# Natural-layout input-projection groups taken two at a time: 512 columns to a PSUM bank, nine buffers of split weights

## The chip, the cores and the metric

The program runs on one core of a Trainium2 chip. The metric is the device time of one execution in microseconds (us), the median of several runs. The profile page and the trace come from one further, profiled execution of the same program.

## The reference

One block of a streaming encoder is computed for 1024 tokens of width 1024, in float32. One input projection feeds three mixers (stick-breaking attention, retention, a Conformer convolution), one output projection and an MLP follow.

```python
h = rms_norm(x, mix_norm_g[l])
u = jnp.einsum('btd,dc->btc', h, w_in[l])            # 1024 -> 3328 columns
sb_q, sb_k, sb_v, r_q, r_k, r_v, r_g, c_a, c_gate = jnp.split(u, split_at, axis=-1)
q = to_heads(rms_norm(sb_q per head of 64), 4); k likewise; v = to_heads(sb_v, 4)
y_sb = from_heads(stick_breaking_attention(q, k, v))
rq = retention_rotary(to_heads(r_q, 8), pos)
rk = retention_rotary(to_heads(r_k, 8), pos) * (HEAD_DIM ** -0.5)
ret = rms_norm(from_heads(multiscale_retention(rq, rk, rv)) per head)
y_ret = jax.nn.silu(r_g) * ret
y_conv = conformer_conv(c_a, c_gate, ...)            # GLU, 31 taps, LayerNorm, silu
x = x + jnp.einsum('btc,cd->btd', concat([y_sb, y_ret, y_conv]), w_out[l])
h = rms_norm(x, mlp_norm_g[l])
x = x + relu(h @ w_ff1[l]) ** 2 @ w_ff2[l]
```

## The kernel before

Every large product is made of three matmuls of a faster float32 form (f32r): each operand is split into a rounded part `hi` and the rest `lo`, and `mm3` adds hi times hi, hi times lo and lo times hi into one PSUM bank. So each weight that comes from memory (`wraw`, 128x512) is first cast on ACT (`whi`, L160) and then subtracted on POOL or DVE (`wlo`, L161). There are `WB` = 6 buffers of each.

The input projection has 13 groups of 256 columns. The first (`qk0`, queries and keys of attention heads 0 and 1) is computed while x arrives and fills all eight banks. Two (`cv0`, `cv1`) are computed in transposed layout, 512 tokens to a bank. The other ten are in natural layout: 128 tokens by 256 columns, eight token tiles `tt` a group, 8 k-steps of 3 matmuls each, in the order v, qk1, then (after the convolution groups) k0, v0, g0, q0, k1, v1, g1, q1. `gemm_group` makes one such group. A token tile fills half a bank of tag "g"; there are two banks of this tag. When the tile is done a function `evac` reads the bank, and only then can the tile after next begin in it: `v_evac` (L307, L308) for v, `sb_norm` and then `sb_turn` for qk1, `rotary` for k and q (two DVE operations L501 and L503, two POOL operations L505 and L506), a copy on ACT for v0 and v1, a sigmoid on ACT and L668 on DVE for g, `ret_chunk` for q.

`ret_chunk` (L586 on) makes one 128-token chunk of retention of four heads: `rotary`, then, a tick later, transposes of k and q on PE (L598, L600) and three copies of them on ACT (L601, L604); scores on PE (L609), masked on DVE (L610); the output on PE (L620, L621) and the state (L627 on PE, L633 or L637 on DVE); a norm; two transposes back (L653).

Small work is laid beside the projection by a count of ticks: `at_tick(t, order, fn)` puts a step at a tick, `tick(gemm)` runs the steps of that tick and then one piece of projection. In before a tick is one token tile of 24 matmuls (of a convolution group one half of a bank, 12 matmuls of 512 columns). A group has 8 ticks: v 0 to 7, qk1 8 to 15, the convolution groups 16 to 31, k0 32 to 39 and so on, to q1 88 to 95. Attention heads begin at tick 1. The 124 convolution taps (`conv_tap`, L533, DVE, 128x512 each) are laid over ticks from 41 on by the list `per`: one a tick for 12 ticks, three for 11, two for 8, then three. A scheduler orders each engine's instructions at build time, starting from this order.

The normalisation factor `rstd` is known only after `qk0` is complete: 8 small matmuls (L224), `mse` on DVE (L225), `rstd` on POOL (L175). Then `sb_norm` of pair 0 runs once for each of the 8 token tiles, each with a POOL operation `rs` (L175) and a DVE multiply into `cv` (L277). `sb_turn` (L284 to L300) transposes four tiles at a time for the attention heads, which begin with z matmuls (L327 to L330), sigmoids on ACT and a scan on DVE (L340).

The weights of the MLP (`wr`, 128x1024, loaded at L828) have four buffers of tag "wr"; one of them serves as `state` of retention until it is over. Three loads of them are issued by SP at the start of the program.

## Time and profile before

| | |
|---|---|
| median of 3 runs | 1163.6 us (1163.55 to 1165.37) |
| profiled execution | 1164.28 us |
| its span in the trace | 1162.5 us |
| PE busy | 1132.3 us (97% of the span) |
| DVE busy | 871.3 us (75%) |
| ACT, POOL busy | 487.5 us, 530.5 us |

The span is the time from the first to the last instruction of the trace; 1.78 us of the profiled execution lie around it, and the median of the runs is 0.68 us below the profiled execution. PE is the engine of the matmuls (TensorE), DVE is VectorE, ACT ScalarE, POOL GpSimd, SP the engine that issues most transfers. Busy time of PE includes the modelled tail of each matmul, so the start-to-start distance of matmuls says more than their own duration.

### The profile page before, as it was taken

Reading aid. Unit: us, or ns where it says so; the run is one execution under the profiler, and the core shown is the slowest. Engines: PE = TensorE matmul, PEld = TensorE weight load, DVE = VectorE, ACT = ScalarE, POOL = GpSimd, SP = SyncE. Lnnn points to the kernel's source line nnn. Section 1 sums busy time; section 2 is a strip of 40 time slices with the busy share of each in tenths; the row PEclk is TensorE's granted clock in tenths of the full one; section 3 lists DMA queues with packets and bytes.
Section 4 is the critical chain, followed back from the end, with each engine's and each line's share of the span. In section 5 each row is a group of like instructions: output and inputs, shape, how many; then the busy total and the mean of one; then the engine's idle time right before and its main releaser. Section 6 shows DMA issues by size and latency. Waiting matters only on the chain.

```text
span 1162.5 us, 17630 instructions
## 1 busy us (share of the span) xinstructions
PE 1132.3 (97%) x6376; PEld 986.6 (85%) x6376; DVE 871.3 (75%) x1355; ACT 487.5 (42%) x921; POOL 530.5 (46%) x432
## 2 busy tenths in 40 slices
PE   7999999999999999999999999999879999999998
PEld 7998889999999998787888888888658888888887
DVE  6786766769987987788966756575588897896964
ACT  7575644442322252555433333343334344344442
POOL 3565535436761562342565655556462442521300
PEclk9999999999999999999999999999989999999999
DMA  8111111112121142212444444453586564553332
GB/s 286 38 37 37 55 29 42 41 55 65 56 65 37 55 182 55 71 66 91 152 146 146 164 141 163 144 163 127 213 311 220 164 212 136 158 183 85 109 129 89
DMA packets 63735, 137.11 MB, mean 118 GB/s; under 512 B 7201, under 2 KB 11937, under 8 KB 63649
## 3 DMA queue, kind: packets, MB, share of 16 engines
q1 hardware_dynamic: 63072, 135.56, 35.5%
q8 instruction: 50, 0.82, 0.3%
q10 hardware_dynamic: 576, 0.44, 0.1%
q14 instruction: 37, 0.29, 0.1%
HBM read 98.22 MB, written 37.75 MB: 117 GB/s over the span
## 4 chain that ended last, share of the span: by engine, by line
PE 84%; DVE 9%; DMA 3%; issue 2%; ACT 1%; SPq 0%; POOL 0%; DVEq 0%; ACTq 0%; POOLq 0%
PE g L116 12%; PE g L118 12%; PE g L117 12%; PE t L117 5%; PE t L118 5%; PE t L116 5%; PE o L117 5%; PE o L116 5%; PE o L118 4%; PE z L117 4%; PE z L118 4%; PE z L116 4%; DVE DM__508_2651 L533 3%; PE o L374 2%; PE t L355 1%
## 5 line engine op out<-in xcount | busy, mean ns | idle before, releaser
L161 DVE TENSOR_TENSOR wlo<-sum,whi 128x512 fp32r<-128x512 f32 x78 | 75.5, 971 | 84.5 <-ACT whi L160 84.5
L161 POOL TENSOR_TENSOR wlo<-wraw,whi 128x512 fp32r<-128x512 f32 x57 | 87.1, 1544 | 77.3 <-ACT whi L160 77.2
L160 ACT CAST whi<-sum 128x512 fp32r<-128x512 f32 x78 | 48.1, 618 | 112.9 <-POOL sum L831 48.1
L161 DVE TENSOR_TENSOR wlo<-wr,whi 128x512 fp32r<-128x512 f32 x80 | 76.6, 963 | 10.0 <-ACT whi L160 9.0
L344 POOL TENSOR_TENSOR be<-be,kp 128x512 f32<-128x512 f32 (+3 forms) x48 | 46.0, 960 | 78.3 <-DVE kp L340 49.9
L160 ACT CAST whi<-wr 128x512 fp32r<-128x512 f32 x80 | 48.5, 620 | 65.5 <-PE t L117 20.8
L836 POOL TENSOR_TENSOR sum<-wr 128x512 f32<-128x512 f32 x16 | 23.2, 1452 | 114.1 <-DMA wr<-in_w_ff_dram 84.1
L160 ACT CAST whi<-wraw 128x512 fp32r<-128x512 f32 x68 | 41.8, 620 | 58.1 <-DMA wraw<-in_w_in_dram 23.5
L340 DVE TENSOR_TENSOR_SCAN kp<-kp 128x512 f32<-128x512 f32 (+3 forms) x48 | 51.1, 1067 | 10.5 <-ACT kp L333 10.0
L533 DVE SCALAR_TENSOR_TENSOR DM__508_2651<-glu,vec,DM__508_2651 128x512 f32<-128x512 f32 x60 | 54.3, 943 | 0.1
L175 POOL TENSOR_TENSOR rs<-ss,nhalf 128x4 f32<-128x4 f32 (+1 forms) x36 | 37.4, 1040 | 30.1 <-DVE ss L641 15.4
L533 DVE SCALAR_TENSOR_TENSOR glu<-glu,vec 128x512 f32<-128x512 f32 x60 | 47.5, 853 | 0.0
L831 POOL TENSOR_TENSOR sum<-wr,sum 128x512 f32<-128x512 f32 x19 | 33.9, 1786 | 11.2 <-DVE wlo L161 11.2
L333 ACT ACTIVATE kp<-z 128x512 f32<-128x512 f32 (+3 forms) x48 | 23.6, 494 | 16.7 <-PE z L330 13.0
L831 POOL TENSOR_TENSOR sum<-sum,wr 128x512 f32<-128x512 f32 x18 | 24.9, 1384 | 11.3 <-DVE wlo L161 11.3
L116 PE MATMUL g<-whi,xh__12_100 128*128 128x256 f32 x82 | 25.3, 309 | 2.8 <-DVE P__107_556 L308 0.9
L334 ACT ACTIVATE be<-z 128x512 f32<-128x512 f32 (+3 forms) x48 | 23.5, 493 | 5.0 <-PE t L355 5.0
L118 PE MATMUL g<-whi,xl__53_362 128*128 128x256 f32 x82 | 23.3, 286 | 1.6 <-DVE xl__53_362 L195 1.6
L116 PE MATMUL g<-whi,xh__34_250 128*128 128x256 f32 x82 | 23.4, 286 | 0.9 <-ACT xh__34_250 L194 0.9
L355 PE MATMUL t<-ident,be 128*128 128x128 f32 x144 | 24.2, 274 | 0.1
L116 PE MATMUL g<-whi,xh__19_145 128*128 128x256 f32 x82 | 23.6, 288 | 0.0
L117 PE MATMUL g<-wlo,xh__19_145 128*128 128x256 f32 x82 | 23.6, 288 | 0.0
(2888 smaller groups left out, 4366.4 us busy)
## 6 DMA issues: line engine op xcount, KB each, us to landing
wr<-in_w_ff_dram SPq DMA_DIRECT2D x40, 512.0 KB, 3.9
wraw<-in_w_in_dram SPq DMA_DIRECT2D x52, 256.0 KB, 3.1
P__418_2109<-in_rot_dram SPq DMA_DIRECT2D x32, 128.0 KB, 2.0
wraw<-in_w_out_dram SPq DMA_DIRECT2D x16, 256.0 KB, 2.7
P__18_143<-in_xT_dram SPq DMA_DIRECT2D x1, 512.0 KB, 4.7
P__22_176<-in_xT_dram SPq DMA_DIRECT2D x1, 512.0 KB, 5.7
P__29_215<-in_xT_dram SPq DMA_DIRECT2D x1, 512.0 KB, 3.5
P__33_248<-in_xT_dram SPq DMA_DIRECT2D x1, 512.0 KB, 7.9
```

What stands on the lines that cost most here:

```text
L116: TE.matmul(out, lh, rh, start=start, stop=False, skip_group_check=on)
L117: TE.matmul(out, lh, rl, start=False, stop=False, skip_group_check=on)
L118: TE.matmul(out, ll, rh, start=False, stop=stop, skip_group_check=on)
L160: S.copy(hi, raw)
L161: (lo_engine or GP).tensor_tensor(out=lo, in0=raw, in1=hi.bitcast(F32), op=ALU.subtract)
L175: GP.tensor_tensor(out=out, in0=in_, in1=nhalf[:, 0:in_.shape[1]], op=ALU.pow)
L333: S.activation(kp[:, 0:n], pz[:, 0:n], AF.Sigmoid, scale=-0.125)
L340: V.tensor_tensor_scan(rev, rev, rev, kp[:, n:n + 1], op0=ALU.mult, op1=ALU.bypass)
L344: GP.tensor_tensor(out=be[:, 0:n], in0=be[:, 0:n], in1=kp[:, 1:n + 1], op=ALU.mult)
L355: TE.transpose(pt[:, j * P:j * P + P], be[:, j * P:j * P + P], ident)
L533: V.scalar_tensor_tensor(out=acc, in0=src, scalar=vec[:, o:o + 1], in1=acc, op0=ALU.mult, op1=ALU.add)
L831: (eng or GP).tensor_tensor(out=o, in0=x, in1=y, op=ALU.subtract)
```

## The change

Ten natural groups become five pairs: v with qk1, k0 with v0, g0 with q0, k1 with v1, g1 with q1. In a pair a weight chunk holds 256 columns of the one and 256 columns of the other group for one k-step, so `mm3` runs on 512 columns and fills a whole bank. A token tile takes two ticks (k-steps 0 to 3, then 4 to 7), so the pair has the same 16 ticks as the two groups had. When the tile is done, both groups' evacuations read their half of the bank.

- The eight chunks of a pair are made by `w_wide`. Nine buffers hold them: the six `whi`/`wlo`, and three 128x1024 tiles `ww` of tag "wr". The `lo` part alternates between DVE and POOL (in before it was on POOL). Raw chunks have five buffers instead of three.
- Before a pair ends, only its last token tile prepares the chunks of the next pair (one is prepared a tile earlier); the pair v with qk1 prepares none.
- Attention heads begin at tick 4 instead of 1, and the third head no longer waits for tick 18.
- `state` moves into a slot of the rotary tables (three slots instead of four for tables), and the buffers of the MLP weights become three of "wr" and one of "wq". The three early loads of MLP weights stand, in SP's order, behind the last rotary table and directly ahead of the eight loads of the residual x; in before they stood between the loads of x at the start.

```diff
-    sources = [d["w_in"][g, :, 512 * c:512 * c + 512] for g in range(len(GROUPS)) for c in range(4)]
+    sources = [d["w_in"][i] for i in range(4 * len(GROUPS))]
     sources += [d["w_out"][i] for i in range(2 * NK)]
     raws = {}
+    rawq = wp.tile([P, 2, 512], F32, tag="wq", name="rawq", bufs=1)
     wpos = [0, 0]
     def w_dma(upto):
         while wpos[0] < min(upto, len(sources)):
-            raw = wp.tile([P, 512], F32, tag="wraw", name=nm("wraw"), bufs=RAW)
+            n = wpos[0] % (RAW + 2)
+            raw = rawq[:, n - RAW, :] if n >= RAW else wp.tile([P, 512], F32, tag="wraw", name=nm("wraw"), bufs=RAW)
             nc.sync.dma_start(raw, sources[wpos[0]])
             raws[wpos[0]] = raw
             wpos[0] += 1
     halves = []
+    nwide = [0]
+
+    def w_wide():
+
+        c = wpos[1]
+        wpos[1] += 1
+        w_dma(c + RAW + (2 if c >= RAW else 0))
+        n = nwide[0] % 9
+        nwide[0] += 1
+        lo_engine = V if nwide[0] % 2 else GP
+        if n < WB:
+            return w_split(raws[c], lo_engine)
+        t = wp.tile([P, 1024], F32R, tag="wr", name=nm("ww"), bufs=3)
+        hi, lo = t[:, 0:512], t[:, 512:1024]
+        S.copy(hi, raws[c])
+        lo_engine.tensor_tensor(out=lo, in0=raws[c], in1=hi.bitcast(F32), op=ALU.subtract)
+        return hi, lo
     def w_part(lo_engine=None):
         if not halves:
             c = wpos[1]
             wpos[1] += 1
-            w_dma(c + RAW)
+            w_dma(c + RAW + (2 if c >= RAW else 0))
             hi, lo = w_split(raws[c], lo_engine)
             halves.extend((hi[:, 256 * h:256 * h + 256], lo[:, 256 * h:256 * h + 256]) for h in range(2))
         return halves.pop(0)
...
     pre = {"w": [], "due": None}
+    AHEAD = {(3, 0): 1}
+
     def gemm_group(evac, ahead=True):
+
         w = pre["w"]
         pre["w"] = []
         for tt in range(NT):
-            def run(tt=tt):
-                while len(w) < NK:
-                    w.append(w_part())
-                ps = bank("g")
-                ts = slice(tt * P, tt * P + P)
-                for k in range(NK):
-                    mm3(ps[:, 0:256], xh[k][:, ts], xl[k][:, ts], w[k][0], w[k][1], k == 0, k == NK - 1)
-                at_tick(now[0] + 1, 0, lambda: evac(tt, ps))
-                if ahead and 2 <= tt and len(pre["w"]) < 2 * WB - NK:
-                    pre["w"].append(w_part())
-            tick(run)
+            pb = {}
+            ts = slice(tt * P, tt * P + P)
+            for kh in range(2):
+                def run():
+                    if kh == 0:
+                        pb[0] = bank("g")
+                    for k in range(4 * kh, 4 * kh + 4):
+                        if len(w) <= k:
+                            w.append(w_wide())
+                        mm3(pb[0], xh[k][:, ts], xl[k][:, ts], w[k][0], w[k][1], k == 0, k == NK - 1)
+                    if ahead and len(pre["w"]) < AHEAD.get((tt, kh), 0):
+                        pre["w"].append(w_wide())
+                    while ahead and tt == NT - 1 and len(pre["w"]) < 4 + 4 * kh:
+                        pre["w"].append(w_wide())
+                tick(run)
+            at_tick(now[0], 0, lambda tt=tt, ps=pb[0]: evac(tt, ps))
     sb_prepare(0)
     mix_sb[0] = page(16)
-    pre["w"] = parts(2 * WB - NK)
     for tt in range(NT):
         sb_norm(0, tt, raw0[tt // 4][:, tt % 4, :])
         if tt % 4 == 3:
             sb_turn(0, tt // 4)
     for i in range(4):
         vst.append(page(12 + i, (P, 2, 4, P), F32R))
-    t1 = sb_head(0, 0, 1)
+    t1 = sb_head(0, 0, 4)
     t1 = sb_head(0, 1, t1)
-    t1 = sb_head(1, 0, max(t1, 18))
+    t1 = sb_head(1, 0, t1)
     sb_end = sb_head(1, 1, t1) + 4
-    gemm_group(v_evac)
     mix_sb[1] = page(17)
     sb_prepare(1)
-    def qk1_evac(tt, ps):
-        sb_norm(1, tt, ps[:, 0:256])
+    def vqk1_evac(tt, ps):
+        v_evac(tt, ps)
+        sb_norm(1, tt, ps[:, 256:512])
         if tt % 4 == 3:
             sb_turn(1, tt // 4)
-    gemm_group(qk1_evac)
+    gemm_group(vqk1_evac, ahead=False)
     rbc = slot("DM")
     at_tick(now[0], 6, lambda: row_bcast(rbc, rstd, "o"))
     glu = [None, None]
...
                         for k in range(4 * kh, 4 * kh + 4):
                             mm3(pb[j], w[k][0][:, cs], w[k][1][:, cs], xh[k][:, tsl], xl[k][:, tsl],
                                 k == 0, k == NK - 1)
-                        if hf == 1 and len(pre["w"]) < 2 * WB - NK:
-                            pre["w"].append(w_part())
+                        if hf == 1 and len(pre["w"]) < (2 * WB - NK if ct == 0 else 3) and (ct == 0 or (j, kh) != (1, 0)):
+                            pre["w"].append(w_part() if ct == 0 else w_wide())
                     tick(run)
             at_tick(now[0], 0, lambda a=(ct, hf, pb[0], pb[1]): conv_gate(*a))
...
     def rot_dma(upto):
         while rpos[0] < min(upto, len(rseq)):
-            nc.sync.dma_start(rott[:, rpos[0] % 4, :], d["rot"][rseq[rpos[0]]])
+            nc.sync.dma_start(rott[:, rpos[0] % 3, :], d["rot"][rseq[rpos[0]]])
             rpos[0] += 1
-    rot_dma(3)
-
-    def rotary(tt, ps, out):
+    rot_dma(2)
+
+    def rotary(tt, ps, out, c0=0):
         n = rpos[1]
         rpos[1] += 1
-        rot_dma(n + 4)
-        tab, c = rott[:, n % 4, :], n % 2
+        rot_dma(n + 3)
+        tab, c = rott[:, n % 3, :], n % 2
         r = rstd[:, tt:tt + 1]
-        src = ps[:, 0:256].rearrange("p (a b) -> p a b", b=2)
+        src = ps[:, c0:c0 + 256].rearrange("p (a b) -> p a b", b=2)
         ma = rotm[:, 2 * c, :].rearrange("p (a b) -> p a b", b=2)
         mb = rotm[:, 2 * c + 1, :].rearrange("p (a b) -> p a b", b=2)
         ov = out.rearrange("p (a b) -> p a b", b=2)
...
         at_tick(c1 + 3 + 2 * t2, 25, lambda t2=t2: conv_norm_b(t2))
     rt = {}
-    state = wp.tile([P, 2, P], F32, tag="wr", name="state", bufs=4)
+    state = rott[:, 3, :].rearrange("p (a b) -> p a b", b=P)
     def ret_chunk(half, c, ps):
         u = c % 2
         kn, vn = rk[c // 4][:, c % 4, :], rv[c // 4][:, c % 4, :]
         qn = rt["q"][:, u, :]
         kT, qT, sT = rt["kT"][:, u], rt["qT"][:, u], rt["sT"][:, u]
-        rotary(c, ps, qn)
+        rotary(c, ps, qn, 256)
         t = now[0]
         def turn():
...
         return fn
     for half in range(2):
-        gemm_group(lambda tt, ps: rotary(tt, ps, rk[tt // 4][:, tt % 4, :]))
-        gemm_group(lambda tt, ps: S.activation(rv[tt // 4][:, tt % 4, :], ps[:, 0:256], AF.Copy,
-                                               scale=rstd[:, tt:tt + 1]))
+        def kv_evac(tt, ps):
+            rotary(tt, ps, rk[tt // 4][:, tt % 4, :])
+            S.activation(rv[tt // 4][:, tt % 4, :], ps[:, 256:512], AF.Copy, scale=rstd[:, tt:tt + 1])
+
+        gemm_group(kv_evac)
         gt[half] = [page(6, (P, 4, 256)), page(7, (P, 4, 256))]
-        gemm_group(g_evac(half))
         if half == 0:
             kq = page(8, (P, 2, 512))
             rt["qT"] = kq[:, :, 0:256].rearrange("p u (a b) -> p u a b", b=P)
...
             rt["dmask"] = page(11, (P, 8, P))
             nc.sync.dma_start(rt["dmask"].rearrange("p a b -> p (a b)"), d["cst"][:, 256:])
         mix_ret[2 * half], mix_ret[2 * half + 1] = (page(14), page(15)) if half == 0 else (page(18), page(19))
-        gemm_group(lambda tt, ps, half=half: ret_chunk(half, tt, ps), ahead=half == 0)
+        g_fn = g_evac(half)
+
+        def gq_evac(tt, ps, half=half, g_fn=g_fn):
+            g_fn(tt, ps)
+            ret_chunk(half, tt, ps)
+
+        gemm_group(gq_evac, ahead=half == 0)
...
     npair = NFT // 2
     raw1, fd, opl = {}, {}, {}
+    nwr = [0]
+
+    def wr_tile():
+        n = nwr[0] % 4
+        nwr[0] += 1
+        return wp.tile([P, 1024], F32, tag="wq" if n == 3 else "wr", name=nm("wr"), bufs=1 if n == 3 else 3)
+
     def load_w1(p):
-        raw1[p] = [wp.tile([P, 1024], F32, tag="wr", name=nm("wr"), bufs=4) for _ in range(2)]
+        raw1[p] = [wr_tile() for _ in range(2)]
         for j in range(2):
             nc.sync.dma_start(raw1[p][j], d["w_ff1"][2 * p + j])
```

The built program shows where steps have moved. Names ending in a number are tiles, numbered anew in each program, and line numbers of the changed program are 2 to 30 higher.

On PE, in the first natural group of before, the first transposes of pair 0 (`sb_turn`, L284, L285) stand between matmuls of the third token tile:

```order
L117 MATMUL g_645<-wlo_438,xh__30_217 128x256
L118 MATMUL g_645<-whi_437,xl__31_218 128x256
L116 MATMUL g_645<-whi_559,xh__34_250 128x256
L117 MATMUL g_645<-wlo_560,xh__34_250 128x256
L118 MATMUL g_645<-whi_559,xl__35_251 128x256
L284 MATMUL t_475<-ident,cv_448 128x128
L285 MATMUL t_476<-ident,cv_448 128x128
L116 MATMUL g_645<-whi_559,xh__41_289 128x256
L117 MATMUL g_645<-wlo_560,xh__41_289 128x256
L118 MATMUL g_645<-whi_559,xl__42_290 128x256
L116 MATMUL g_645<-whi_565,xh__45_322 128x256
```

In the change the same transposes stand (as L305, L306) behind the whole second token tile, here with the last matmuls of the bank `g_633`, and the third tile (`g_679`) begins only after two turns and the first four z products (L348 to L351):

```order
L118 MATMUL g_633<-ww_616,xh__52_364 128x512
L119 MATMUL g_633<-ww_616,xh__52_364 128x512
L120 MATMUL g_633<-ww_616,xl__53_365 128x512
L305 MATMUL t_466<-ident,cv_439 128x128
L306 MATMUL t_467<-ident,cv_439 128x128
L305 MATMUL t_466<-ident,cv_439 128x128
L306 MATMUL t_467<-ident,cv_439 128x128
...
L348 MATMUL z_761<-P__61_427,P__59_425 128x512
L350 LDWEIGHTS identb
L350 MATMUL z_761<-maskb,identb 128x128
L351 MATMUL z_761<-P__60_426,P__59_425 128x512
L118 MATMUL g_679<-whi_557,xh__12_101 128x512
```

What moved: two whole tiles of 512 columns, 48 matmuls, now stand ahead of the small work that followed `rstd`, and no projection matmul stands inside that work. On DVE, the multiply of `sb_norm` for pair 1 (L298), which is the last reader of the first bank `g_555`, stands behind the turn of pair 0 and the first two scans (L361):

```order
L298 TENSOR_TENSOR cv_512<-P__57_401,rs_519 128x256
L291 TENSOR_REDUCE ss_662<-e_133_660 128x4
L292 TENSOR_SCALAR ss_626<-ss_626,ceps 128x4
L357 MEMSET kp_697 128x1
L321 CAST P__63_429<-P__64_430 64x512
L361 SCALAR_TENSOR_TENSOR kp_673<-kp_673 128x128
L292 TENSOR_SCALAR ss_662<-ss_662,ceps 128x4
L361 SCALAR_TENSOR_TENSOR kp_697<-kp_697 128x256
L298 TENSOR_TENSOR cv_631<-g_555,rs_629 128x256
L357 MEMSET kp_737 128x1
```

Its factor `rs_629` is on POOL the ninth of its kind, behind the eight of pair 0 (of which three stand here):

```order
L196 TENSOR_TENSOR rs_502<-ss_499,nhalf 128x4
L196 TENSOR_TENSOR rs_510<-ss_507,nhalf 128x4
L196 TENSOR_TENSOR rs_519<-ss_516,nhalf 128x4
L196 TENSOR_TENSOR rs_629<-ss_626,nhalf 128x4
L365 TENSOR_TENSOR be_672<-be_672,kp_673 128x128
L196 TENSOR_TENSOR rs_665<-ss_662,nhalf 128x4
```

In before the bank's only readers at this place were the two operations of `v_evac`, which need no `rs`. On PE, in q0 of before, the transposes of a chunk (into `t_3745`) stand beside the scores of the chunk ahead of it (`z_3739`), whose own transposes stand 18 projection matmuls earlier:

```order
L598 MATMUL t_3745<-ident,P__415_2106 128x128 x2
L600 MATMUL t_3745<-ident,P__598_3306 128x128 x2
L621 MATMUL o_3715<-P__416_2107,P__600_3308 128x64 x2
L620 MATMUL o_3715<-state,P__598_3306 128x128
L621 MATMUL o_3715<-P__416_2107,P__600_3308 128x64 x2
L609 MATMUL z_3739<-P__598_3306,P__599_3307 128x128 x4
L116 MATMUL g_3843<-whi_3434,xh__19_145 128x256
L117 MATMUL g_3843<-wlo_3435,xh__19_145 128x256
```

In the change, in the pair g0 with q0, the transposes L626 and L628 (into `t_2960`) and the scores L637 of the same chunk (`z_2991`) follow one another, with no projection matmul between them:

```order
L649 MATMUL o_2936<-P__378_1828,P__525_2531 128x64 x2
L681 MATMUL t_2931<-ident,e_584_2875 128x128 x2
L626 MATMUL t_2960<-ident,P__376_1826 128x128 x2
L628 MATMUL t_2960<-ident,P__523_2529 128x128 x2
L648 MATMUL o_3018<-P__380_1830,P__523_2529 128x128
L637 MATMUL z_2991<-P__523_2529,P__524_2530 128x128
L655 MATMUL z_3027<-P__378_1828,P__376_1826 128x128 x2
L637 MATMUL z_2991<-P__523_2529,P__524_2530 128x128 x3
L118 MATMUL g_3082<-ww_2143,xh__12_101 128x512
L119 MATMUL g_3082<-ww_2143,xh__12_101 128x512
```

What moved: the small work of a chunk is gathered at the boundary of two token tiles, ahead of the 24 matmuls of the next bank. This form stands at 8 of the 16 chunks.

## Rows read from the trace of the kernel before

**Rows 1.** The page, parts 1 and 2: busy time, tenths of 40 slices.
```profile
PE 1132.3 (97%) x6376; PEld 986.6 (85%) x6376; DVE 871.3 (75%) x1355; ACT 487.5 (42%) x921; POOL 530.5 (46%) x432
...
PE   7999999999999999999999999999879999999998
```
**Rows 2.** Windows by stage: us, busy of each engine (instructions), clock, DMA share, GB/s.
```profile
236.30:296.50 60.20, 59.81 (x507) 59.60 (x506) 50.67 (x84) 19.06 (x44) 32.12 (x29) 1.00 0.22 64
...
358.40:424.00 65.60, 63.95 (x532) 62.94 (x531) 54.26 (x93) 21.16 (x51) 31.19 (x31) 1.00 0.23 74
```
**Rows 3.** Waits of PE, 38 to 450: total us, times, longest.
```profile
PE g L116 <- DVE P__107_556 L308: 0.9, 1, 0.9
PE g L116 <- DVE P__419_2110 L503: 0.8, 1, 0.8
...
PE o L620 <- DVE state L637: 0.2, 1, 0.2
```
**Rows 4.** Timeline of PE in g0: start, duration, instruction.
```profile
239.80 0.28 PE L117 MATMUL g<-wlo,xh__41_289 128*128 128x256 f32 x1
...
240.76 0.28 PE L117 MATMUL g<-wlo,xh__45_322 128*128 128x256 f32 x1
```
**Rows 5.** Timeline of PE in the output projection, 512 columns.
```profile
499.62 0.39 PE L118 MATMUL o<-xh__947_5700,wlo 128*128 128x512 f32 x1
...
501.44 0.39 PE L117 MATMUL o<-P__964_5773,whi 128*128 128x512 f32 x1
```
**Rows 6.** Waits of PE, 0 to 37, behind the fourth load of x.
```profile
PE g L118 <- DVE xl__53_362 L195: 1.6, 1, 1.6
PE g L116 <- ACT xh__34_250 L194: 0.9, 1, 0.9
```
**Rows 7.** Window of the start, same columns as Rows 2.
```profile
0.00:20.00 20.00, 13.49 (x79) 13.20 (x80) 12.13 (x20) 12.44 (x17) 5.73 (x7) 1.00 0.86 291
```
**Rows 8.** Timeline of PE: the matmuls for rstd.
```profile
38.38 1.84 PE L224 MATMUL t<-ones,P__1_84 128*128 128x1 f32 x16
```
**Rows 9.** Timeline of POOL after rstd (first and last; 8 rs).
```profile
40.51 1.65 POOL L175 TENSOR_TENSOR rstd<-mse,nhalf 128x8 f32<-128x8 f32 x1 [0.28 <-DVE mse L225]
...
48.08 3.44 POOL L175 TENSOR_TENSOR rs<-ss,nhalf 128x4 f32<-128x4 f32 x3 [0.22 <-DVE ss L271]
```
**Rows 10.** Timeline of DVE from mse to the first scans.
```profile
52.46 0.43 DVE L277 TENSOR_TENSOR cv<-P__57_398,rs 128x256 f32<-128x256 f32 x1
...
56.77 1.20 DVE L340 TENSOR_TENSOR_SCAN kp<-kp 128x128 f32<-128x128 f32 x2 [0.49 <-ACT kp L333]
```
**Rows 11.** Timeline of DVE: three taps in g0, three in q0.
```profile
257.82 2.07 DVE L533 SCALAR_TENSOR_TENSOR DM__508_2651<-glu,vec,DM__508_2651 128x512 f32<-128x512 f32 x3
...
274.70 2.58 DVE L533 SCALAR_TENSOR_TENSOR DM__508_2651<-glu,vec,DM__508_2651 128x512 f32<-128x512 f32 x3
```
**Rows 12.** Instructions of DVE by line, 236.3 to 296.5: count, busy us, mean ns.
```profile
L501 DVE SCALAR_TENSOR_TENSOR P__419_2110<-g,rstd,P__418_2109 128x256 f32<-128x256 f32 x7 | 3.3, 474 | 0.0
...
L610 DVE TENSOR_TENSOR P__600_3308<-z,P__601_3311 128x512 f32<-128x512 f32 x3 | 2.0, 681 | 0.0
L668 DVE SCALAR_TENSOR_TENSOR P__559_2991<-g,rstd,e 128x256 f32<-128x256 f32 x4 | 1.9, 484 | 5.1 <-ACT e L667 5.0
...
L637 DVE SCALAR_TENSOR_TENSOR state<-state,vec,z 64x64 f32<-64x64 f32 x7 | 1.8, 276 | 0.0
...
L645 DVE TENSOR_TENSOR e<-o,rs 128x256 f32<-128x256 f32 x2 | 0.8, 410 | 0.0
```
**Rows 13.** Timeline of ACT: the three copies of one chunk.
```profile
272.19 0.38 ACT L601 COPY P__598_3306<-t 128x256 f32<-128x256 f32 x1 [4.34 <-PE t L600]
272.45 0.76 ACT L604 COPY P__599_3307<-t 64x256 f32<-64x256 f32 x2
```
**Rows 14.** The page, part 5: splits of weights on DVE, on POOL.
```profile
L161 DVE TENSOR_TENSOR wlo<-wr,whi 128x512 fp32r<-128x512 f32 x80 | 76.6, 963 | 10.0 <-ACT whi L160 9.0
...
L161 POOL TENSOR_TENSOR wlo<-wraw,whi 128x512 fp32r<-128x512 f32 x57 | 87.1, 1544 | 77.3 <-ACT whi L160 77.2
```

More of the change, by code (lines that the diff above doesn't have):

```diff
@@ L28 @@
 GROUPS = ["qk0", "v", "qk1", "cv0", "cv1", "k0", "v0", "g0", "q0", "k1", "v1", "g1", "q1"]
+WIDE = {1: "v", 5: "k0", 7: "g0", 9: "k1", 11: "g1"}
 V_MIX, V_MLP, V_GQ, V_GK, V_RET, V_PWA, V_PWG = 0, 8, 16, 17, 18, 22, 24
@@ L151, in w_quarter @@
             wpos[1] += 1
-            w_dma(c + RAW)
+            w_dma(c + RAW + (2 if c >= RAW else 0))
             hi, lo = w_split(raws[c], lo_engine)
@@ L940, in load_w2 @@
             nw2[0] += 1
-            t = wp.tile([P, 1024], F32, tag="wr", name=nm("wr"), bufs=4) if tag == "wr" else slot(tag)
+            t = wr_tile() if tag == "wr" else slot(tag)
             load(t, d["w_ff2"][2 * p + j])
@@ L1083 @@
     w_in = np.asarray(inputs["w_in"])[0][:, _columns()]
-    w_in = w_in.reshape(NK, P, 13, 256).transpose(2, 1, 0, 3).reshape(13, P, 2048)
+    w_in = w_in.reshape(NK, P, 13, 256).transpose(2, 1, 0, 3)
+    srcs = []
+    for g in range(13):
+        if g in WIDE:
+            srcs += [np.concatenate([w_in[g, :, k], w_in[g + 1, :, k]], axis=1) for k in range(NK)]
+        elif g - 1 not in WIDE:
+            srcs += [w_in[g, :, 2 * c:2 * c + 2].reshape(P, 512) for c in range(4)]
+    w_in = np.stack(srcs)
     rows = np.concatenate([np.arange(0, 512), np.arange(768, 1024), np.arange(512, 768)])
```

## The prediction

> **What bounds the kernel now.** I read the page's busy times first. PE is busy in 97% of the span and in nearly every slice, DVE in 75% [rows 1]. So a microsecond taken from PE's stream counts, if nothing makes PE wait for it. The windows by stage come next: in the pair g0, q0 and in the pair g1, q1 DVE is busy 50.67 of 60.20 us and 54.26 of 65.60 us [rows 2]. There DVE is the next engine in line. The waits of PE from 38 to 450 us are few, nine rows from 0.9 us down to 0.2 us [rows 3], some 4 us together. Matmuls are read by their starts: in g0 eight steps of 256 columns take 0.96 us, 0.120 us each [rows 4]; in the output projection eight steps of 512 columns take 1.82 us, 0.2275 us each [rows 5]. Small matmuls: in g0 and q0 there are 507, of which 2 x 8 x 24 = 384 are of 256 columns. They take 46.1 us, and the other 123 have 14.1 us, 0.115 us each [rows 2, 4].
>
> **A. The stream, -12.0 us.** Ten groups of 8 tiles of 24 matmuls are 1920 of 256 columns; they become 960 of 512. A pair cost 0.240 us and one wide matmul costs 0.2275, so 12.5 ns are saved 960 times. The count of weight loads halves too, but they run beside the matmuls, so I give nothing for that.
>
> The Trainium skill, "TensorE: Matmul & The Clock Gate", section "Back-to-back issue gap", gives a warm gap of N/2.4 + 2.5 ns. By that (estimate from the page) a pair saves only 2.5 ns, 2.4 us in all, and the sum would come out 9.6 us higher. The rows show longer steps than the page's 109 and 216 ns, and 12.5 ns between them, so I take the rows.
>
> **B. The start, -2.5 us.** Three loads of MLP weights, 1.5 MB, leave the place between the loads of x; two more raw chunks, 0.5 MB, come in ahead of the fifth load of x. So 1.0 MB less stands ahead of it. The start moves 291 GB/s [rows 7], hence 3.4 us. PE waits 0.9 and 1.6 us for work on the last four loads of x [rows 6], 2.5 us. I take 2.5, bounds 0 (the loads of x also wait for their three pages) and 3.4.
>
> **C. Old waits at bank releases, -2.0 us.** The two largest waits of PE, 0.9 us for `v_evac` and 0.8 for `rotary` [rows 3], are at group boundaries that no longer exist in that form. With a part of the smaller ones I take 2, bounds 0 and 2.5.
>
> **D. The first wide pair, +6 us.** The bank `g_555` is now released by `sb_norm` of pair 1, not by `v_evac` alone. That multiply stands on DVE behind pair 0's eight multiplies, one turn and two scans, and its factor is the ninth `rs` on POOL. In before, PE begins v 13 matmuls ahead of the first matmul for `rstd`, at 38.38 - 1.56 = 36.82 us [rows 4, 8]. In the change 20 wide matmuls stand ahead of it, 4.55 us in place of 1.56, so everything from `rstd` on is 2.99 us later against the start of the group.
> - Upper bound: in before the same list on DVE, to the end of the second scan, is over at 56.77 + 1.20 = 57.97 us [rows 10]. With the multiply itself, 0.43 [rows 10], and the 2.99 that is 61.4, 24.6 us after the group's start.
> - Lower bound: the eighth `rs` ends at 48.08 + 3.44 = 51.52 [rows 9]. A ninth (3.44 / 3 = 1.15), the multiply and the 2.99 give 56.1, 19.3 us after the start.
> - PE's work until it needs the bank: 48 wide matmuls, 10.9 us; the matmuls for `rstd`, 1.84 [rows 8]; 16 transposes at 0.115, 1.8; the z products and masks, by the step of 256 columns about 1.3. Together 15.8 us.
>
> So PE stands between 3.5 and 8.8 us. The turn was held up in before by projection matmuls between its transposes, and is not now, so the list ends earlier than the upper bound; I take 6. Queued behind the waiting matmul is the rest of PE, so all of it counts.
>
> **E. Retention in two pairs, +8 us.** Two things happen at the tile boundaries. First, at 8 of 16 chunks the scores follow their own transposes with a matmul or so between (once five). The three copies on ACT between them run from 272.19 to 272.45 + 0.76 = 273.21, 1.02 us [rows 13]. In before 18 or so projection matmuls covered that. Eight times 1.02, less some 0.15 of PE work each, is 7 us. Second, a tile of the wide pair has, on DVE, six taps at 0.69 (2.07 / 3) to 0.86 (2.58 / 3) us [rows 11], 4.1 to 5.2 us; the gate 0.48, `rotary` 0.95, the mask 0.68, four state updates 1.1, two 256-wide operations of the norm 0.82 [rows 12]; and 0.6 `lo` splits at 0.96 that were on POOL [rows 14]. That is 8.6 to 9.7 us. PE has 24 x 0.2275 = 5.5 and about 18 small ones, 2.1: 7.5 us. DVE falls behind by 1.1 to 2.2 us a tile, over five tiles with three taps a tick (30 taps stand between five evacuations in the order of DVE) 5 to 11 us in each pair. Two banks let DVE be late by most of a tile, and the standing for the copies gives DVE time, so most of this is not added. I take 8: the 7 and 1 more. Bounds: 2, if PE comes to the transposes late enough or DVE's lateness and the copies fall together with other small work; 18, if a lag of 8 to 9 us in each pair goes through.
>
> **F. The rest, +0.5 us.** At a boundary of pairs a chunk's cast on ACT and split on POOL (1.54 us, [rows 14]) follow the last use of a buffer. Each chunk has three matmuls of a tile's 24 between its predecessor's release and its own use, and with nine buffers some 5 us of cover; gone, it would cost about 2 us at a boundary. The three MLP loads ahead of the residual loads are hidden by the last tiles of q1 and the start of the output projection, which doesn't read x at once. Bounds 0 and 4. The third and fourth attention heads only move; no engine gets more of them.
>
> **The sum.** -12.0 - 2.5 - 2.0 + 6 + 8 + 0.5 = -2.0. Against the profiled execution, 1164.28 us (span 1162.5, 1.78 around it), that is 1162.3. The median of the runs shown is 0.68 lower, so I predict 1161.6 against 1163.6. A difference of 0.2%, 2.3 us, is about what a measurement of this kernel can tell from no change.
>
> **Rivals.**
> 1. *The new waits are mostly covered.* Then D is 3.5, E 2, F 0 and B 3.4: -12.0 - 3.4 - 2.0 + 3.5 + 2 = -11.9, 1151.7 us. For it: DVE has 9.5 us to spare over g0 and q0, and 11.3 over g1 and q1 [rows 2]. Against it: the order of PE leaves nothing between transposes and scores.
> 2. *DVE bounds both retention pairs.* The lag goes through, E is 17, and the sum is +7.0, 1170.6 us. It decides from E = 12.3 on, since all else sums to -10.0 and 2.3 must be left. For it: taps beside POOL's work take 0.86 us and not 0.69 [rows 11], and more splits come to DVE. Against it: the total of DVE stays under the total of PE in both pairs.
> 3. *A wide matmul saves little beside 256 columns here.* If the step were not 0.2275 but 0.2375, as when weight loads of this stream hold it, A would be 2.4 and the sum +7.6, 1171.2 us. The skill's gap named under A would give the same. Against it stand rows 4 and 5, both of this program.
>
> **How the numbers follow.** My forecast has 0.50, with a range of its own from 1157 to 1166; of this 0.24 lie more than 0.2% under before, 0.21 within, 0.05 above. Rival 1 has 0.22, all faster. Rival 2 has 0.22: 0.19 slower and 0.03 the same. Rival 3 has 0.06, slower. Together faster 0.46, same 0.24, slower 0.30. The bounds of the terms sum to -12.0 - 3.4 - 2.5 + 3 + 2 = -12.9 and to -12.0 + 9 + 18 + 4 = +19; for 8 in 10, up to the two rivals' times, I take 1150 to 1172.
>
> **What would show it.** A: starts 0.2275 us apart in the wide pairs. B: v begins before 36.82 us. D: PE waits several us for DVE's `cv` (L298) at its third tile, and nowhere else as long. E: waits of PE of about 1 us for ACT's copies at eight scores, or long waits for `rotary` at the first matmul of a tile; in the second case rival 2 is right. F: no wait for `wlo` over 1 us at the first tile of a pair. The prediction is wrong if the wait in D is hidden or exceeds 9 us, if the retention pairs lose more than 12 us, or if a cost appears in a stage that I give none, the output projection above all.

## The result and the profile after

The change made the kernel slower: 1175.3 us median (1172.95 to 1176.29) against 1163.76 us (1163.55 to 1165.37), a ratio of 1.0094, interval 1.0081 to 1.0108. I had forecast 1161.6 us in a range up to 1172. The span grew from 1162.5 to 1174.5 us. Busy times and clock of the page after, to be read beside [rows 1]:

```profile
PE 1128.8 (96%) x5416; PEld 938.7 (80%) x5416; DVE 889.1 (76%) x1375; ACT 480.4 (41%) x921; POOL 515.7 (44%) x412
...
PE   7799999999899989999999999999979999999998
...
PEclk9899999999999999999999999999979999999999
```

The clock's row of the page before:

```profile
PEclk9999999999999999999999999999989999999999
```

PE has 960 matmuls less. Its busy time fell by only 3.5 us; that time also holds the stretches at a lower granted clock that are shown below. The view of cores gives a mean granted clock of 0.985 (0.994 before).

The stages tell where the time went. Each boundary is the first matmul of a stage; the numbers are differences of starts in the traces, and the last column is the best kernel of the experiments (run e7). The MLP is counted from the first matmul of its norm.

| stage, us | before | after | difference | e7 |
|---|---|---|---|---|
| to the start of v | 36.82 | 33.91 | -2.9 | 34.26 |
| v, qk1, convolution groups | 133.64 | 136.76 | +3.1 | 127.86 |
| k0, v0 | 65.79 | 64.36 | -1.4 | 64.12 |
| g0, q0, k1, v1 | 122.15 | 130.62 | +8.5 | 125.40 |
| g1, q1, output projection | 182.65 | 188.78 | +6.1 | 180.81 |
| MLP | 621.45 | 620.07 | -1.4 | 619.45 |

Two places lose. The waits of PE from 40 to 450 us, to be read beside [rows 3], name both:

```profile
PE o L648 <- ACT P__523_2529 L629: 7.4, 6, 3.7
PE o L648 <- DVE P__380_1830 L665: 4.2, 1, 4.2
PE z L348 <- DVE P__61_427 L318: 3.7, 1, 3.7
PE t L305 <- DVE cv L298: 2.8, 2, 1.9
PE g L118 <- DVE P__381_1831 L531: 1.5, 2, 0.8
```

The first two rows are retention (L648 is the first matmul of its output, L629 the copy of q on ACT, L665 the state on DVE): 11.6 us. The next two are attention's turn and first z. The last row, a bank waiting for `rotary`, is where DVE as the bound would have shown; it is small.

**The first pair.** The timelines of PE and DVE, and the windows with the granted clock in the column after the busy times:

```profile
48.55 0.27 PE L306 MATMUL t<-ident,cv 128*128 128x128 f32 x1
52.51 0.47 PE L348 MATMUL z<-P__61_427,P__59_425 128*128 128x128 f32 x1 [3.68 <-DVE P__61_427 L318]
...
58.06 0.78 PE L351 MATMUL z<-P__60_426,P__59_425 128*128 128x512 f32 x1
```
```profile
57.36 0.75 DVE L361 TENSOR_TENSOR_SCAN kp<-kp 128x256 f32<-128x256 f32 x1
58.14 0.42 DVE L298 TENSOR_TENSOR cv<-g,rs 128x256 f32<-128x256 f32 x1
```
```profile
45.00:50.00 5.00, 2.93 (x17) 2.09 (x15) 3.45 (x12) 2.49 (x7) 3.84 (x4) 1.00 0.01 2
50.00:55.00 5.00, 2.04 (x8) 1.39 (x8) 4.79 (x11) 4.72 (x8) 2.22 (x3) 0.56 0.00 0
55.00:60.00 5.00, 5.00 (x16) 3.73 (x17) 4.74 (x14) 3.53 (x10) 3.40 (x4) 0.50 0.00 0
```

The multiply that frees the first bank ends at 58.56, and the third tile begins at 58.63, directly behind the z matmuls that the order of PE has ahead of it. The waits view shows 3.7 us for L318, on which the first of these z matmuls waits. So the small work and the bank were ready within 0.1 us of each other, and this trace alone does not say which of them held the tile. The copies below (e1) show that the reader of the bank is behind both: without it the order has the third tile ahead of the z matmuls, and the tile begins 10 us earlier. PE was idle for most of 48.8 to 52.5, and then the granted clock was about 0.5, which is the level of 1.2 GHz, to the end of these windows.

**Retention.** One tile boundary in g0, q0, and the stand at the pair's end, on PE, ACT and DVE:

```profile
284.56 0.39 PE L120 MATMUL g<-whi,xl__53_365 128*128 128x512 f32 x1
284.79 0.55 PE L649 MATMUL o<-P__378_1828,P__525_2531 128*128 128x64 f32 x4
...
286.29 0.38 PE L628 MATMUL t<-ident,P__523_2529 128*128 128x128 f32 x2
287.62 0.49 PE L648 MATMUL o<-P__380_1830,P__523_2529 128*128 128x128 f32 x2 [0.95 <-ACT P__523_2529 L629]
...
289.22 0.48 PE L118 MATMUL g<-ww,xh__12_101 128*128 128x512 f32 x1
```
```profile
310.30 0.80 PE L648 MATMUL o<-P__380_1830,P__523_2529 128*128 128x128 f32 x2 [3.74 <-ACT P__523_2529 L629]
```
```profile
305.98 0.62 ACT L181 CAST whi<-wraw 128x512 fp32r<-128x512 f32 x1 [2.48 <-DMA wraw<-in_w_in_dram]
...
308.20 0.62 ACT L181 CAST whi<-rawq 128x512 fp32r<-128x512 f32 x1 [0.95 <-DMA rawq<-in_w_in_dram]
...
309.35 0.62 ACT L181 CAST whi<-rawq 128x512 fp32r<-128x512 f32 x1
309.86 0.38 ACT L629 COPY P__523_2529<-t 128x256 f32<-128x256 f32 x1
```
```profile
305.44 2.42 DVE L561 SCALAR_TENSOR_TENSOR DM__464_2241<-glu,vec,DM__464_2241 128x512 f32<-128x512 f32 x2
307.79 1.28 DVE L182 TENSOR_TENSOR wlo<-wraw,whi 128x512 fp32r<-128x512 f32 x2
308.99 0.77 DVE L665 SCALAR_TENSOR_TENSOR P__380_1830<-P__380_1830,vec,z 64x64 f32<-64x64 f32 x3
```

From the last transpose to the output matmul 1.33 us pass, of which 0.95 stand in the row. At the pair's end the same matmul stands 3.74 us: the copy it needs comes on ACT behind casts that waited for loads, and the state it also needs comes on DVE behind two taps and two splits. Both were done within half a microsecond of each other, at 310.24 and 309.76.

The second long stand, in g1, q1, is different:

```profile
435.84 0.46 PE L648 MATMUL o<-P__380_1830,P__523_2529 128*128 128x128 f32 x2 [4.15 <-DVE P__380_1830 L665]
```
```profile
432.76 0.40 ACT L629 COPY P__523_2529<-t 128x256 f32<-128x256 f32 x1
```
```profile
431.78 3.42 DVE L740 TENSOR_TENSOR xl__838_4504<-P__528_2537,xh__837_4503 128x512 fp32r<-128x512 f32 x2
435.13 0.77 DVE L665 SCALAR_TENSOR_TENSOR P__380_1830<-P__380_1830,vec,z 64x64 f32<-64x64 f32 x3
```

Here the copy is done at 433.16. The state comes last, on DVE behind splits of the output projection's inputs (L740), and DVE alone holds PE for the last 2.7 us of the 4.15.

Both long stands are at the sixth of the eight chunks of their half. In the second half the transposes of k of chunks five to eight, which read tile `P__377`, begin at 421.41, 431.07, 442.44 and 452.34, and the stand follows the second of them; in the first half it is the same.

### The profile page after: what moved, and what is told of

It is laid out like the page before. It is cut to its first block, busy times and chain, and to the rows that moved or that the text cites. A ratio compares the mean times of both kernels' runs of the same rounds, so it can differ in the third digit from the quotient of the medians.

```text
span 1174.5 us, 15670 instructions
## 1 busy us (share of the span) xinstructions
PE 1128.8 (96%) x5416; PEld 938.7 (80%) x5416; DVE 889.1 (76%) x1375; ACT 480.4 (41%) x921; POOL 515.7 (44%) x412
## 4 chain that ended last, share of the span: by engine, by line
PE 72%; DVE 12%; issue 7%; POOL 5%; DMA 3%; ACT 2%; POOLq 0%; SPq 0%; DVEq 0%; ACTq 0%
PE g L118 11%; PE g L120 11%; PE g L119 10%; PE o L119 4%; PE o L120 4%; PE o L118 4%; PE t L120 4%; PE t L119 4%; PE t L118 4%; PE z L120 3%; PE z L119 3%; PE z L118 3%; DVE wlo L182 2%; PE o L395 1%; POOL sum L873 1%
## 5 line engine op out<-in xcount | busy, mean ns | idle before, releaser
L182 DVE TENSOR_TENSOR wlo<-sum,whi 128x512 fp32r<-128x512 f32 x78 | 78.6, 1011 | 88.5 <-ACT whi L181 88.5
L361 DVE TENSOR_TENSOR_SCAN kp<-kp 128x512 f32<-128x512 f32 (+3 forms) x48 | 54.8, 1150 | 10.0 <-ACT kp L354 9.6
L561 DVE SCALAR_TENSOR_TENSOR DM__464_2241<-glu,vec,DM__464_2241 128x512 f32<-128x512 f32 x60 | 49.1, 855 | 0.0
L354 ACT ACTIVATE kp<-z 128x512 f32<-128x512 f32 (+3 forms) x48 | 23.7, 495 | 33.7 <-PE z L351 21.8
L182 POOL TENSOR_TENSOR wlo<-wraw,whi 128x512 fp32r<-128x512 f32 x18 | 28.6, 1596 | 12.4 <-ACT whi L181 12.4
L182 POOL TENSOR_TENSOR wlo<-rawq,whi 128x512 fp32r<-128x512 f32 x13 | 22.3, 1721 | 16.7 <-ACT whi L181 16.7
L181 ACT CAST whi<-wraw 128x512 fp32r<-128x512 f32 x33 | 19.9, 618 | 13.6 <-DMA wraw<-in_w_in_dram 8.0
L376 PE MATMUL t<-ident,be 128*128 128x128 f32 x144 | 24.6, 275 | 0.6 <-POOL be L365 0.4
L648 PE MATMUL o<-P__380_1830,P__523_2529 128*128 128x128 f32 x56 | 12.4, 304 | 11.6 <-ACT P__523_2529 L629 7.4
L533 POOL TENSOR_TENSOR P__523_2529<-P__381_1831 128x128 f32<-128x128 f32 x16 | 15.0, 939 | 18.6 <-DVE P__381_1831 L531 18.6
L873 POOL TENSOR_TENSOR wr<-wr,wr 128x512 f32<-128x512 f32 x16 | 22.5, 1404 | 1.2
L651 ACT ACTIVATE e<-o 128x256 f32<-128x256 f32 x16 | 6.1, 383 | 38.1 <-PE o L649 38.0
```

The source lines that it names most:

```text
L181: S.copy(hi, raw)
L182: (lo_engine or GP).tensor_tensor(out=lo, in0=raw, in1=hi.bitcast(F32), op=ALU.subtract)
L361: V.tensor_tensor_scan(rev, rev, rev, kp[:, n:n + 1], op0=ALU.mult, op1=ALU.bypass)
L376: TE.transpose(pt[:, j * P:j * P + P], be[:, j * P:j * P + P], ident)
L561: V.scalar_tensor_tensor(out=acc, in0=src, scalar=vec[:, o:o + 1], in1=acc, op0=ALU.mult, op1=ALU.add)
L873: (eng or GP).tensor_tensor(out=o, in0=x, in1=y, op=ALU.subtract)
```

## Experiments

Each kernel is the changed one with one edit, unless said otherwise. Its ratio is to the kernel before, run on the same chip (medians 1163.8 to 1164.6).

**e1: the qk1 half of the first four banks copied to SBUF by ACT; `sb_norm` reads the copy.**

```diff
+    rawd = slot("DM", (P, 4, 256))
     def vqk1_evac(tt, ps):
         v_evac(tt, ps)
-        sb_norm(1, tt, ps[:, 256:512])
+        src = ps[:, 256:512]
+        if tt < 4:
+            S.copy(rawd[:, tt, :], src)
+            src = rawd[:, tt, :]
+        sb_norm(1, tt, src)
```

> The changed kernel, in which the qk1 half of the first four wide banks is copied to SBUF by ACT and sb_norm reads the copy; v_evac and the copy are then the only readers of the bank, as v_evac alone was before. Theory (the third tile stands because the bank waits for the normalisation of pair 1): the third tile begins at about 45 us instead of 58.6, the granted clock stays 1.00 there, v with qk1 takes 60 to 62 us instead of 69.2, and the total falls by 7 to 9 us to 1166 to 1168 us. Rival (the long list after rstd on POOL and DVE bounds the stage whoever reads the bank, and the standing only moves to the attention heads' first z or to the turns of pair 1): the stage loses less than 3 us and the total is 1172 us or more.

Measured 1175.37 us, ratio 1.0100 (1.0085 to 1.0115): no gain in the total. The third tile did begin earlier, 48.43 in place of 58.63, and the clock stayed 1.00 there. But the later tiles, not copied, waited for the same multiply (L298), and the start of this execution was 1.6 us later. From the start of v to k0 it took 132.9 us, 3.9 less than after. Its third tile and its waits:

```profile
48.43 0.48 PE L118 MATMUL g<-whi,xh__12_101 128*128 128x512 f32 x1
```
```profile
PE g L118 <- DVE cv L298: 3.7, 2, 1.8
PE o L255 <- DVE cv L253: 1.2, 2, 0.8
```

**e4: all chunks of retention later.**

```diff
-        at_tick(t + 1, 14, turn)
-        at_tick(t + 2, 13, scores)
-        at_tick(t + 3, 12, out)
-        at_tick(t + 5, 11, back)
+        at_tick(t + 2, 14, turn)
+        at_tick(t + 4, 13, scores)
+        at_tick(t + 5, 12, out)
+        at_tick(t + 7, 11, back)
```

> The changed kernel, in which retention's turn is one tick later, scores and output two ticks later, so that projection matmuls stand between a chunk's transposes and its scores on PE at all 16 chunks. Theory (PE stands for the three copies on ACT, and twice for 4 us, when ACT or DVE has other work queued ahead at a pair's end): PE's waits at the output of retention, 11.6 us, fall under 3, and the total falls by 8 to 11 us to 1164 to 1167 us. Rival (DVE bounds the retention pairs: 6 taps and all evacuations in a tile): the waits reappear at the first projection matmul of a tile, for rotary or the gate, tiles of g0 and q0 still take 9 to 10 us, and the total changes by less than 3 us.

Measured 1162.0 us, ratio 0.998 (0.9971 to 0.9989): 13.3 us less than the change, and a little under the kernel before. Between the transposes and the scores of a chunk 8 to 39 projection matmuls stand now in the order of PE, at all 16. Its largest waits at the same places:

```profile
PE g L118 <- DVE P__381_1831 L531: 1.8, 2, 1.0
PE o L649 <- DVE P__525_2531 L638: 1.1, 1, 1.1
PE o L648 <- DVE P__380_1830 L665: 0.8, 1, 0.8
```

The 11.6 us of L648 are 0.8, with 1.1 at L649, the other matmuls of the output. The wait of a bank for `rotary` went from 1.5 to 1.8 only. DVE has the same work as after. So the amount of DVE's work was not the bound of these pairs; the place of the transposes beside the matmuls that wait for copy and state was.

**e6: both edits.**

> Both edits together. If the two waits are the whole loss and independent, the gains add: 1175.3 - 8 - 9.5 = 1157 to 1159 us, below the 1163.8 of the kernel before. If DVE bounds retention, it is near the first edit's time alone, 1166 to 1169.

Measured 1161.45 us, ratio 0.9979 (0.9967 to 0.9992). The gains did not add, as four copies bring nothing.

**e2: g0, q0, g1, q1 single again** (`WIDE` without 7 and 11, the group loop of before for these four).

> The changed kernel with g0, q0, g1, q1 again as single groups of 256 columns, the other three pairs wide. Theory: the retention losses of about 15 us go, and 4 x 8 x 24 / 2 x 0.0125 = 4.8 us of stream come back: 1164 to 1167 us. If a wide group as such (its buffers, its splits on DVE) costs, and not the order of retention's work, the gain is under 5 us.

Measured 1167.5 us, ratio 1.0036 (1.0021 to 1.0050), 7.8 us less than the change. With e4 this says that retention's loss can be had back without giving up the wide banks.

**e9 and e10: e4's ticks for the last chunk of each half alone (`c == NT - 1`), and for all the others alone.**

> The changed kernel; only the last chunk of each half of retention has its transposes one tick and its scores and output two ticks later. Theory (two different losses: at a pair's end the copies on ACT stand behind casts of the next chunks of weights, and the state update on DVE behind splits, 4 us each; elsewhere the three copies alone, about 1 us each): the two waits of 3.7 and 4.2 us go, the six of about 1 us stay, and the total falls by 6 to 8 us to 1167 to 1169 us. Rival (all is one loss, DVE too late): the wait moves to the chunk ahead or to a bank and the total falls by less than 3 us.

> The changed kernel; all chunks of retention but the last of each half have the later ticks. Theory: the waits of about 1 us at six boundaries go, the two of about 4 us stay, and the total falls by 5 to 7 us to 1168 to 1170 us; with the run on the last chunk alone it adds up to the 13.3 us that the shift of all chunks gave. Rival: the whole 13.3 us come with these chunks, 1162 us.

Measured 1178.46 us for e9, ratio 1.0124 (1.0109 to 1.0139), and 1160.89 for e10, ratio 0.9979 (0.9967 to 0.9992). The two do not share the gain as expected: all of it is with the other chunks, and my picture of the last chunk was wrong. The long stands belong to the sixth chunk, which e10 moves and e9 does not. In e9 they are where they were, one now put down to the norm's sum on DVE:

```profile
PE o L648 <- DVE P__380_1830 L665: 4.2, 1, 4.2
PE o L648 <- DVE ss L668: 3.7, 1, 3.7
```

What e9 loses beside the change comes later: from the end of the second stand to the MLP it takes 123.1 us, the change 118.6. In the output projection it has a wait of 1.7 us for DVE (L831) that the change has not, and a granted clock of 0.83 in the 10 us from 486, where the change has 1.00.

**e11: the ticks for the last chunk but one alone (`c == NT - 2`).**

> The changed kernel; only the last chunk but one of each half has the later ticks. By the order this parts its transposes from its scores in the second half (18 projection matmuls between) and not in the first (still none). The run on the last chunk alone showed that the two stands of about 4 us stay when that chunk is moved, so they should belong to the chunk ahead of it. Then the stand of 4.2 us in the second half goes, the one of 3.7 us in the first stays, and the total is 1170.5 to 1172.5 us. If it moves on once more, 1174 to 1177 us.

Measured 1174.95 us, ratio 1.0088 (1.0071 to 1.0105): the stand in the second half stayed, 4.1 us. That says nothing of its cause: it is the sixth chunk's again, with two more pairs of transposes behind it in PE's order, and this run moves the seventh.

**e15: no chunks prepared in the last tile of g0, q0** (`ahead=False`). This also takes away the one chunk that `AHEAD` prepares early, in the fourth of the eight tiles, and not, as The change has it, one tile before the last.

> The changed kernel; the last tile of g0 with q0 prepares no chunks of k1 with v1, which are then made in that pair's first tile. Theory for the stand of 3.7 us at the end of g0, q0 (the copies wait on ACT behind the casts of those chunks, and the casts for their loads): the stand shrinks to about 1 us, and the first tile of k1, v1 pays instead, as its eight chunks can be split no faster than one in about 1.5 us on POOL or 1 on DVE while PE needs one in 0.7. If the stand stays at over 3 us, the casts are not its cause.

Measured 1175.86 us, ratio 1.0103 (1.0086 to 1.0119). It tells nothing of the casts: the scheduler put them where they had been, and the order of PE, ACT, DVE and POOL is that of the change word for word. It is a second measurement of the change, 0.6 us from the first.

**e7: all chunks later, and all eight qk1 halves copied** (`rawd[:, tt % 4, :]`, for every `tt`).

> All chunks later, and the qk1 half of all eight banks of the first pair copied to SBUF. If the banks of the later tiles, which still wait for the normalisation on DVE when only four are copied, are what gave the first copy's gain back, the waits of 3.7 us at a bank's first matmul go and the total is 1157 to 1159 us. If the attention heads' own chain is what fills the time up to the convolution groups, it is 1161 to 1163 us, as with four copies (1161.5) and none (1162.0).

Measured 1153.5 us (1152.98 to 1155.3), ratio 0.9912 (0.9895 to 0.9928), the fastest median of all and 8.5 us under e4. No bank waits for the normalisation any more; what is left is small:

```profile
PE g L118 <- DVE P__382_1840 L537: 1.8, 2, 1.0
PE t L305 <- DVE P__219_1082 L379: 1.6, 1, 1.6
PE o L255 <- DVE cv L253: 1.4, 1, 1.4
```

**e16: the eight copies alone, retention as in the change.**

> The changed kernel with all eight qk1 halves of the first pair copied to SBUF, retention's ticks as in the change. If the first pair's loss is separate from retention's, the gain is that seen on top of the later ticks, 1162.0 - 1153.5 = 8.5 us: 1166 to 1168 us. If four copies' failure (1175.4) repeats, the gain depends on retention's order.

Measured 1169.02 us (1165.55 to 1171.7), ratio 1.0038 (1.0026 to 1.0051): 6.3 us less than the change. The first pair's loss stands by itself.

**e8: all chunks later, v and qk1 single.**

> All chunks later, and v and qk1 as single groups of 256 columns. If the wide first pair costs what its stand measured net (5.6 us lost, 2.4 us of stream saved), 1162.0 - 3.2 = 1158 to 1160 us. If the attention heads' chain bounds this stretch whatever the width, it is 1161 to 1164 us.

Measured 1154.27 us, ratio 0.9919 (0.9904 to 0.9934). The single groups recover what the copies recover, 7.7 us of e4, so the wide first pair as it was cost that much net.

**e12: only k0, v0 and k1, v1 wide.**

> The changed kernel with only k0, v0 and k1, v1 wide; v, qk1, g0, q0, g1, q1 are single groups, retention's ticks as in the change. What is left of the change is the start, two wide pairs with light evacuations and the attention heads' new ticks. By the steps: start -2.9, stream 2 x 2.4 = -4.8, no stands: 1163.8 - 7.7 = 1155 to 1157 us. If wide groups cost something of their own (their buffers and splits), it is 1159 us or more.

Measured 1159.67 us, ratio 0.9957 (0.9942 to 0.9971): 4.9 us under the kernel before in the same runs, 3 less than the sum. By the trace the stages from v to g0 take 7.8 us less than before, and those from g0 to the MLP 7.1 more: g0, q0, k1, v1 126.68 us (122.15 before), and g1, q1 and the output projection 185.26 (182.65 before), these last in waits of banks below 1 us each. The first of the two is there in e14 too, without any wide group. The cause of the second I leave open.

**e14: the kernel before, with attention heads from tick 4 and no wait for tick 18.**

> The kernel before with one part of the change alone: the attention heads begin at tick 4, and the third does not wait for tick 18. My prediction gave this part nothing: 1163 to 1165 us. The run with the first groups narrow spent 4.2 us less between the start of v and k0 than the kernel before; if the heads' ticks are the cause and not only move the work behind k0, it is 1159 to 1161 us.

Measured 1163.83 us, ratio 0.9993 (0.9983 to 1.0002): nothing, as predicted. Its trace has 4.4 us less from v to k0 and 5.2 more from k0 to the MLP. So the heads' ticks move work behind k0, and the first rows of e7 in the table of stages hold this shift as well.

**e13: eight copies, and all chunks but the last later.**

> The two edits that gained most together: all eight qk1 halves copied, and every chunk of retention but the last of each half later. By the sum of what they gave apart, 1153.5 and -1.1: 1152 to 1153 us. If it is no faster than 1153.5, the last chunk's ticks are of no account.

Measured 1154.26 us, ratio 0.9910 (0.9895 to 0.9924). No faster than e7.

## Why the prediction was wrong

- **A, the stream: right in the step, 1.6 us too large in the sum.** In the wide pairs eight steps take 1.82 us, 0.2275 each, so rival 3 falls:

```profile
282.06 0.39 PE L118 MATMUL g<-whi,xh__33_250 128*128 128x512 f32 x1
...
283.88 0.39 PE L120 MATMUL g<-whi,xl__44_322 128*128 128x512 f32 x1
```

Not every step is such a one. Added up in the traces from start to start, less waits over 0.15 us, the ten groups take 237.0 us in before and 226.6 in e7, so A gave 10.4 and not 12.0. The formula that A takes from the Trainium skill, "TensorE: Matmul & The Clock Gate", section "Back-to-back issue gap", is given there for an isolated matmul; the steps of this stream, 0.120 and 0.2275 us, are 11 to 12 ns longer than its 109 and 216 ns.

- **B, the start: right.** v begins 2.9 us earlier; I took 2.5. In other runs the gain was between 1.3 and 3.3 (v from 33.5 to 35.5 us), with waits of 1 to 3 us at other places of the start. In e14, whose start is that of before, v began at 38.1, so an execution differs from the next by over 1 us here.
- **C, old waits: wrong.** The waits for `v_evac` at a bank are gone; those for `rotary` grew from 0.8 to 1.5 us [rows 3], and others came. Even in e7, where the losses of D and E are gone, PE waits 9.5 us between v and the MLP, in rows of at most 1.8 us and most of them for DVE; in before it is 4.0.
- **D, the first pair: right in mechanism (e1, e7, e16), its size at the upper bound.** The third tile begins 24.7 us after the pair's start; the upper bound of the bank's release was 24.6. I had taken an earlier end. The copies alone gave 6.3 us back and 8.5 on top of e4, beside the 6 of the sum. I had not counted the lower clock behind the stand.
- **E, retention: the step that failed, in its size.** I took 8; the waits at the output are 11.6 us, and e4 gave back 13.3. With the long stands the granted clock fell, which the waits do not hold: it was 0.80 from 305.0 to 313.3, around the first, and 0.76 from 435.84 to 443.0, behind the second. The part "Eight times 1.02, less some 0.15" was too much if anything: five such stands, 3.7 us together, none over 1.0. What was missing are the two stands of 3.7 and 4.2 us. I had priced the copies as if they began when the transposes end, and did not ask what stands ahead of them on ACT, and ahead of the state on DVE, at a pair's end, where the chunks of the next pair and the splits of the output projection's inputs are made. The same work stood in F, where I called it hidden with 0.5 us: it was hidden from the chunks' own matmuls, whose wait for `wlo` is 0.3 us, and not from those of retention.
- The other half of E, DVE falling behind by 1.1 to 2.2 us a tile, did not happen. PE's small work in a tile is 3.3 us (284.79 to 289.22, less 1.1 of standing), not the 2.1 that I worked out: with 5.5 of projection a tile takes PE 8.9 us, about what DVE needs. Rival 2 named the right stages and the right side (1170.6 us), by a mechanism that e4 refutes: what DVE held up is the state at one chunk, and not the banks of every tile.
- The gains as a whole were over-counted. e4 took away 13.3 us and the eight copies on top 8.5, together 21.8; with both losses gone e7 is 10.3 us under the kernel before. A, B, C and F together claimed 16.0. About 6 us of that are missing; by the stages e7 saves 6.0 us between the start of v and the MLP, where A and C claimed 14. Of these, A's sum is short by 1.6 and C by 7.5, as its waits grew by 5.5 in place of falling by 2.0. Some 3 us won elsewhere stand against it, 2.0 of them in the MLP, to which I gave no term. A first wide step behind small work is long, 0.31 us (279.21 to 279.52) and not 0.2275, but a first step of 256 columns is as much longer (0.20 for 0.12), so this takes nothing from A.
- So of the 13.7 us between forecast and result some 5 are E, 2.5 D (by the 8.5 of its copies) and 6 the gains. Two sums of the prediction are a little off, without weight for this: D's lower bound enters the sum of the bounds as 3 and not 3.5, and DVE's items for a tile add up to 8.7 to 9.8 us.

**What stays open.** For the second long stand the trace names DVE with its splits, as the copy was there 2.7 us earlier. For the first, ACT with its casts and DVE with taps and splits were late at the same moment, and no run parts them: none moves the sixth chunk alone (e9 and e11 move others), and the run that should have taken the casts away did not change the order (e15). Open is also what puts the wait and the lower clock into the output projection of e9.

## What to carry to other kernels

When two pieces of work come to share a PSUM bank, the bank is freed by the slower of the two: look for what stands on every engine's queue ahead of that last reader, and if it is long, copy the half out first (e7). When a step is made twice as long, steps counted in ticks come to stand side by side: check in the order that a transpose and the matmul that needs its copy have work between them (e4). Price such a pair at the place where the queues of the engines it waits for are fullest, not at an average tile. And before a run that moves one step, find in the trace which step it is that stands (e9, e11).

## What was not expected

After PE had stood for 4 us with little small work around it (48.55 to 52.51), the granted clock was 0.56 in the window from 50 to 55 us and 0.50 in the next, although PE was busy all through that one. In the start of e1, with a PE wait of 1.9 us early on, it was 0.79 in the window from 12 to 20 us. With the stand removed the clock of the first pair was 1.00 throughout, as the windows of e7 show:

```profile
34.20:48.00 13.80, 13.80 (x72) 11.66 (x72) 4.73 (x17) 5.98 (x18) 6.88 (x6) 1.00 0.08 21
48.00:86.90 38.90, 38.90 (x198) 32.13 (x197) 31.60 (x74) 27.02 (x59) 17.45 (x18) 1.00 0.03 7
```
